# Two-block transformer kernel on one core: order of emission in the gated delta net's pair loop

## Chip, cores and metric

One core of a Trainium2 chip runs the whole program; times are device microseconds of that core. TensorE (PE in the profile) multiplies, VectorE (DVE) and ScalarE (ACT) work on tiles, GpSimd (POOL) does small side work, SyncE (SP) issues most transfers.

## What is computed

Two transformer blocks one after the other on x of 512 tokens by 1024 features. The first has dilated attention and retention, cross attention and a gated MLP. The second takes h = modulated norm of x, and hc the same of 256 context tokens, and runs a gated delta net (GDN) and latent attention (MLA) side by side, merges them and adds an MLP. The change is in the GDN: 8 heads of 128, in both directions, over chunks (of 128 tokens in the kernel, 6 of them: 2 of context, 4 of x). The core of the reference:

```python
qkv = jax.nn.silu(_centred_conv(qkv, conv_w))          # 5 taps
q, k = _l2norm(q), _l2norm(k)
...
diff = gc[..., :, None] - gc[..., None, :]
decay = jnp.where(tri, jnp.exp(jnp.where(tri, diff, 0.0)), 0.0)
a_mat = jnp.where(strict, jnp.einsum('bhnid,bhnjd->bhnij', kb, k) * decay, 0.0)
t_mat = lax.linalg.triangular_solve(eye + a_mat, jnp.broadcast_to(eye, a_mat.shape), ...)
u = jnp.einsum('bhnij,bhnjd->bhnid', t_mat, vb)
w = jnp.einsum('bhnij,bhnjd->bhnid', t_mat, kb * jnp.exp(gc)[..., None])
qk = jnp.where(tri, jnp.einsum('bhnid,bhnjd->bhnij', q, k) * decay, 0.0)
...
def step(s, inp):
    v_new = u_i - jnp.einsum('bhcd,bhde->bhce', w_i, s)
    o_i = einsum(qd_i, s) + einsum(qk_i, v_new)
    s = s * gl_i[..., None, None] + einsum(kd_i, v_new)
...
y = _rms(o, w_norm) * jax.nn.silu(z)
```

## The kernel before

Products of weights are made in three parts (`mm3s`): each operand is a high and a low half, and a product of one 128-feature tile with the 512 tokens of x is 24 instructions of 512 columns on lines 234, 235 and 237 (8 blocks of 128 rows, three parts each); with the 256 context tokens 24 of 256 columns. Weight halves come in two ways. Keys, queries and values have theirs laid ready in memory ("parts") and only load them (`whi<-parts`). Those of z and of all that follows load raw (`wraw`); ACT makes whi (L178), DVE wlo (L179). Both ways have two buffers of each name. The 512-column results go to two banks `pg`, others to four banks `sc` and two `pt`.

`gdn` goes over four pairs of heads, numbered 0 to 3. A pair's work, by the names used below:

- keys, queries (512 columns only) and values: two feature tiles each. A tile's product is evacuated twice by ACT (L1247, L1248), DVE adds the four other taps of the conv (`conv`, L1254, 510/511 or 254/255 columns), ACT applies silu (L1256). Keys and values are turned (L1284; evacuated on L1286, L1289), keys and queries get their norms (L1309, L1322, L1325). `betas` takes the logarithm of the key norms (L1341).
- the within-chunk part, first half of `states`: products of keys with keys and queries (L1364, L1366), a decay mask per direction from two small products (L1373, L1374) through an exponential on ACT (L1376), products with it on DVE (L1378 to L1380), and the diagonal 32x32 blocks of all into X (L1384, L1386).
- the inversion, on DVE alone: a transpose of X (L1390), 31 steps of small multiplications and subtractions (L1398, L1401, some 124 instructions), two transposes back (L1403, L1404).
- TT: small products on PE that put the inverse of the blocks together (L1418 to L1456); then the recurrence of six steps (L1475 to L1527), in which PE, DVE and ACT wait for each other at each step. L1502 is the last product of a step.
- `output`: z's two products, their silu (L1535), the norm of O (L1542 to L1547), O turned on PE (L1550) and multiplied with z (L1552).

SP runs in program order. On the other engines a list scheduler sets the order: it takes the instructions by a planner's costs, and among those that are ready what was emitted first goes first. So the order in which the code emits a pair's parts decides what fills PE while DVE inverts. Before, the loop emits: TT, recurrence and all before it of pair p (`states`), then keys, queries and values of pair p + 1 (`inputs`), `betas`, then z and the output of pair p. In the last pass `tail()` stands in place of the next inputs: it holds the latent projections of MLA (256-column weight pieces, loaded raw; results evacuated on L980) and gates. The list of the calls:

```python
*inp, n2 = inputs(0)
g = next(gg)
...
for pair in range(4):
    O = states(pair, *inp, *bt)
    ...
    output(pair, O, sq_)
```

`gg` is a generator of the decay gates (`gdn_gates`, L1150 on), of which `inputs(0)` takes the first stage between its query norms and the turn of its values.

Of the kernel before, what the change touches and what calls it, by code (L numbers as in the profile page):

```python
# [75 lines left out]
class Kernel:  # L76
# [1155 lines left out]
    def gdn(self, H, HC, w, tail):  # L1232
# [8 lines left out]
        def conv(ps, tile):  # L1241

            raw, acc = (self.page([sum(p.shape[1] for p in ps)]) for _ in range(2))
            o = 0
            for p in reversed(ps):
                n = p.shape[1]
                act(raw[:, o:o + n], p, AF.Copy)  # L1247
                act(acc[:, o:o + n], p, AF.Copy, scale=cw[:, 48 + tile:49 + tile])  # L1248
                for i in (0, 1, 3, 4):
                    wi = cw[:, 24 * i + tile:24 * i + tile + 1]  # L1250
                    a, b = max(0, 2 - i), min(n, n + 2 - i)
                    y = acc[:, o + a:o + b]
                    v = raw[:, o + a + i - 2:o + b + i - 2]
                    dve.scalar_tensor_tensor(y, v, wi, y, op0=OP.mult, op1=OP.add)  # L1254
                o += n
            act(acc, acc, AF.Silu)  # L1256
            return acc, raw
# [11 lines left out]
        def feat(f0, both, first=None):  # L1269

            W, pc = first or (None, None)
            W = W or self.weights(w, 0, 8, f0, 256)
            for f in range(2):
                r = [product(W, H, f, 512, "pg")]
                if both:
                    r.append(pc[f] if pc else product(W, HC, f, 256, "pg"))
                yield r
# [15 lines left out]
        def inputs(pair):  # L1293


            h0 = 2 * pair
            qT, sq_, kT, ktok, vtok = ([] for _ in range(5))
            fk = fv = None
            if pair == 0:
                fv = None, ahead(2048)[1]  # L1300
                fk = ahead(1024)
            kc = [conv(ps, 8 + h0 + f) for f, ps in enumerate(feat(1024 + pair * 256, True, fk))]
            n2, root = [], []
            for f, (c, raw) in enumerate(kc):
                kt = self.page([6, 128])
                turn(c, kt)
                ss = self.tmp.tile([128, 6], F32, name="kss")
                for t in range(6):
                    act(raw[:, t * 128:t * 128 + 128], kt[:, t], AF.Square, accum_out=ss[:, t:t + 1])  # L1309
                n2.append(self.hb.tile([128, 6], F32, name=f"kn2{f}", bufs=2))  # L1310
                root.append(self.hb.tile([128, 6], F32, name=f"krt{f}", bufs=2))
                nc.gpsimd.tensor_scalar(n2[f], ss, 1e-6, None, op0=OP.add)
                r = self.hb.tile([128, 6], F32, name="krs", bufs=2)
                nc.gpsimd.tensor_tensor(r, n2[f], self.mhalf[:, :6], op=OP.pow)
                nc.gpsimd.tensor_tensor(root[f], r, n2[f], op=OP.mult)
                kT.append(c.rearrange("p (a b) -> p a b", a=6))
                ktok.append(kt)
            qc = [conv(ps, h0 + f) for f, ps in enumerate(feat(pair * 256, False))]
            vc = [conv(ps, 16 + h0 + f) for f, ps in enumerate(feat(2048 + pair * 256, True, fv))]
            for q, sq in qc:  # L1320
                qT.append(q)
                act(sq, q, AF.Square)  # L1322
                pq = self.bank([128, 4], "pt")
                for t in range(4):
                    mm(pq[:, t:t + 1], sq[:, t * 128:t * 128 + 128], ones, start=True, stop=True)  # L1325
                s1 = self.tmp.tile([128, 4], F32, name="qss")
                dve.tensor_copy(s1, pq)
                sq_.append(self.rstd(s1, 1.0 / 128, 128e-6, "qrs"))
            if pair == 0:
                next(gg)  # L1330
            for f, (c, _) in enumerate(vc):
                vt = self.page([6, 128])
                turn(c, vt, root[f])
                vtok.append(vt)
            return qT, sq_, kT, ktok, vtok, n2

        def betas(pair, n2):
            h0, nb, bd = 2 * pair, [], []
            for f in range(2):
                ln = self.hb.tile([128, 6], F32, name="kln", bufs=2)  # L1340
                act(ln, n2[f], AF.Ln)  # L1341
                inv = self.hb.tile([128, 6], F32, name="kin", bufs=2)
                dve.reciprocal(inv, n2[f])
                for out, nm, v, op in ((nb, "nb", ln, OP.subtract), (bd, "bd", inv, OP.mult)):
                    out.append(self.hb.tile([128, 6, 2], F32, name=f"k{nm}{f}", bufs=2))
                    dve.tensor_tensor(out[f], g[nm][:, :, h0 + f::8], v[:, :, None].to_broadcast([128, 6, 2]), op=op)
            return nb, bd

        def states(pair, qT, sq_, kT, ktok, vtok, nb, bd):
            h0 = 2 * pair  # L1350
            D2 = range(2)
            lane = {(h, d): slice(12 * h + 6 * d, 12 * h + 6 * d + 6) for h in D2 for d in D2}

            def blk(b):
                return slice(32 * b, 32 * b + 32)


            E, M = {}, {}
            for h in range(2):
                pg = [self.bank([128, n, 128], "sc") for n in (2, 4)]  # L1360
                pk = self.bank([128, 4, 128], "sc")
                for c in range(6):
                    k = kT[h][:, c]
                    mm(pg[c >= 2][:, c - 2 * (c >= 2)], k, k, start=True, stop=True)  # L1364
                    if c >= 2:
                        mm(pk[:, c - 2], k, qT[h][:, (c - 2) * 128:(c - 1) * 128], start=True, stop=True)  # L1366
                for d in range(2):
                    i = d * 8 + h0 + h
                    ec, e = self.page([2, 128], s="w"), self.page([4, 128], s="w")
                    for a, n in ((0, 2), (2, 4)):  # L1370
                        pe = self.bank([128, n, 128], "sc" if a else "pt")
                        pf = pe.rearrange("p a b -> p (a b)")
                        mm(pf, sel[:, i:i + 1].to_broadcast([64, 128]), g["rows"][:, a * 128:(a + n) * 128], start=True, stop=False)  # L1373
                        mm(pe, idb, msk[:, d, None, :].to_broadcast([128, n, 128]), start=False, stop=True)  # L1374
                        for c in range(n):
                            act((e if a else ec)[:, c], pe[:, c], AF.Exp, bias=nb[h][:, a + c, d:d + 1])  # L1376
                    m = self.page([6, 128], s="w")
                    dve.tensor_tensor(m[:, :2], ec, pg[0], op=OP.mult)  # L1378
                    dve.tensor_tensor(m[:, 2:], e, pg[1], op=OP.mult)
                    dve.tensor_tensor(e, e, pk, op=OP.mult)  # L1380
                    for b in range(4):
                        xb, mb = X[blk(b), lane[h, d]], m[blk(b), :, blk(b)]
                        if d == 0:
                            act(xb, mb, AF.Copy)  # L1384
                        else:
                            dve.transpose(xb, mb)  # L1386
                    E[h, d], M[h, d] = e, m


            dve.transpose(L, X.rearrange("p n i -> p i n"))  # L1390
# [15 lines left out]

            pairs = [[(2 * p + d, 2 * p + 1 - d) for p in D2] for d in D2]
            h1 = [slice(64 * d, 64 * d + 64) for d in D2]
            h2 = h1[::-1]
            V, TT, pa, P, pb = ([None, None] for _ in range(5))  # L1410
            for h in D2:
                V[h] = [[R[:, lane[h, d]] for R in ((R1, R2), (R2, R1))[d]] for d in D2]
                pa[h] = self.bank([128, 6, 32], "sc")
                for c in range(6):
                    for p in D2:
                        for d in D2:
# [46 lines left out]
            O = [self.page([4, 128], s="w") for h in range(2)]  # L1463
            for s in range(6):
# [22 lines left out]
                for h in range(2):  # L1487
                    if s < 5:
                        vd[h] = self.hb.tile([128, 2, 128], F32, name="gvd", bufs=2)
                        f = bd[h].rearrange("p c d -> p (c d)")[:, lo:hi + 1:hi - lo]  # L1490
# [63 lines left out]
                self.dbg(f"d_o{h0 + h}", f)  # L1554

        gg = self.gdn_gates(H, HC, w)
        *inp, n2 = inputs(0)
        g = next(gg)
        g = next(gg)
        bt = betas(0, n2)  # L1560
        for pair in range(4):
            O = states(pair, *inp, *bt)
            sq_ = inp[1]
            if pair < 3:
                *inp, n2 = inputs(pair + 1)
                bt = betas(pair + 1, n2)
            else:
                tail()
            output(pair, O, sq_)
# [54 lines left out]
```

## Time and profile before

| | us |
|---|---|
| median of three runs (2303.47 to 2306.6) | 2304.15 |
| the profiled execution | 2301.69 |
| its span, first to last instruction | 2299.6 |
| PE busy in the span | 2180.8 (95%) |
| DVE busy | 1193.7 (52%) |
| ACT busy | 990.1 (43%) |
| POOL busy | 255.3 (11%) |

The mean granted TensorE clock over the span is 0.984 of full speed. The page's slices show PE at nine tenths or more nearly everywhere; the GDN stands from about 940 to 1480 us. Busy shares over the whole span hide which engine ends a wait, so the rows further down are of that stretch.

### The profile page before, as it was taken

What the parts mean: (1) busy time and instruction counts of PE and PEld (TensorE: products, weight loads), DVE (VectorE), ACT (ScalarE), POOL (GpSimd) and SP (SyncE); (2) the same over time, 40 slices, a digit from 0 to 9 for tenths busy, and PEclk for the clock granted to TensorE, in tenths of its full rate; (3) what the DMA queues carried; (4) which work ended last, traced back from release to release, by engine and by line L of the source; (5) the groups of instructions that cost most, each with busy time, mean ns of one, the idle gap of its engine ahead of it and who ended that gap; (6) DMA issues with size and microseconds to landing.
All of it is one profiled execution on the core that took longest, in us unless ns stands there. A gap on an engine that the chain in (4) does not pass through costs nothing.

```text
span 2299.6 us, 38173 instructions
## 1 busy us (share of the span) xinstructions
PE 2180.8 (95%) x15367; PEld 1941.2 (84%) x15367; DVE 1193.7 (52%) x2628; ACT 990.1 (43%) x2054; POOL 255.3 (11%) x419
## 2 busy tenths in 40 slices
PE   8999999998899999888989897999999998999999
PEld 8889978888779889767878786888988898898988
DVE  4554444555443233559696867336775454434343
ACT  4443234545333233565555654445555324313231
POOL 0221100001000001201111110211210001010112
PEclk9999999999999999999999998999999998999999
DMA  5233485455663322422121310230112442323232
GB/s 173 80 128 130 159 290 194 158 183 183 216 231 104 101 92 97 152 80 93 47 92 47 98 47 15 90 120 28 30 51 92 165 147 74 101 83 101 93 100 92
DMA packets 195816, 262.05 MB, mean 114 GB/s; under 512 B 12343, under 2 KB 157495, under 8 KB 195639
## 3 DMA queue, kind: packets, MB, share of 16 engines
q1 hardware_dynamic: 188864, 244.61, 33.0%
q10 hardware_dynamic: 6775, 15.00, 1.8%
q8 instruction: 120, 1.97, 0.3%
q14 instruction: 57, 0.47, 0.1%
HBM read 223.39 MB, written 36.18 MB: 113 GB/s over the span
## 4 chain that ended last, share of the span: by engine, by line
PE 74%; issue 9%; DMA 5%; DVE 5%; ACT 4%; POOL 2%; ACTq 0%; SPq 0%; POOLq 0%; DVEq 0%
PE pg L234 15%; PE pg L235 15%; PE pg L237 15%; PE sc L234 4%; PE sc L237 4%; PE sc L235 4%; DMA whi<-parts 2%; DMA parts<-fraw 1%; PE pg L223 1%; PE pg L224 1%; PE pg L225 1%; PE pa L1148 1%; PE sc L465 1%; DMA wraw<-in_w_kv_mem 1%; PE sc L1486 1%
## 5 line engine op out<-in xcount | busy, mean ns | idle before, releaser
L179 DVE TENSOR_TENSOR wlo<-wraw,whi 128x1024 fp32r<-128x1024 f32 (+2 forms) x267 | 325.7, 1222 | 415.2 <-ACT whi L178 411.3
L234 PE MATMUL pg<-xhi,whi 128*128 128x512 f32 (+1 forms) x1104 | 426.9, 390 | 32.5 <-DMA whi<-parts 13.4
L178 ACT ACTIVATE whi<-wraw 128x1024 fp32r<-128x1024 f32 (+2 forms) x267 | 275.5, 1034 | 417.7 <-PE pg L235 352.2
L235 PE MATMUL pg<-xlo,whi 128*128 128x512 f32 (+1 forms) x1104 | 424.9, 388 | 0.0
L237 PE MATMUL pg<-xhi,wlo 128*128 128x512 f32 (+1 forms) x1104 | 291.2, 384 | 0.9 <-DMA wlo<-parts 0.9
L234 PEld LDWEIGHTS pg<-xhi,whi 128*128 128x128 f32 x1104 | 210.5, 191 | 79.6 <-ACT whi L178 14.4
L235 PEld LDWEIGHTS pg<-xlo,whi 128*128 128x128 f32 x1104 | 210.7, 191 | 37.0
L237 PEld LDWEIGHTS pg<-xhi,wlo 128*128 128x128 f32 x1104 | 202.7, 190 | 41.2 <-DMA wlo<-parts 3.1
L234 PE MATMUL pg<-whi,xhi 128*128 128x256 f32 (+1 forms) x608 | 158.8, 291 | 0.3 <-ACT a L980 0.3
L235 PE MATMUL pg<-whi,xlo 128*128 128x256 f32 (+1 forms) x608 | 157.0, 289 | 0.0
L234 PE MATMUL sc<-whi,a 128*128 128x256 f32 x560 | 141.7, 285 | 1.6 <-ACT whi L178 1.6
L235 PE MATMUL sc<-whi,a 128*128 128x256 f32 x560 | 141.2, 284 | 0.0
L234 PE MATMUL pg<-whi,a 128*128 128x256 f32 x560 | 140.9, 283 | 0.0
L235 PE MATMUL pg<-whi,a 128*128 128x256 f32 x560 | 140.8, 283 | 0.0
L234 PEld LDWEIGHTS pg<-whi,xhi 128*128 128x128 f32 x608 | 118.4, 195 | 4.5 <-ACT whi L178 2.5
L235 PEld LDWEIGHTS pg<-whi,xlo 128*128 128x128 f32 x608 | 118.2, 194 | 1.1 <-issue 0.8
L237 PE MATMUL pg<-wlo,xhi 128*128 128x256 f32 (+1 forms) x608 | 103.2, 289 | 14.4 <-DVE wlo L179 14.4
L234 PEld LDWEIGHTS sc<-whi,a 128*128 128x128 f32 x560 | 107.7, 192 | 2.0 <-ACT whi L178 1.8
L235 PEld LDWEIGHTS sc<-whi,a 128*128 128x128 f32 x560 | 107.7, 192 | 0.2
L234 PEld LDWEIGHTS pg<-whi,a 128*128 128x128 f32 x560 | 107.5, 192 | 0.2
L235 PEld LDWEIGHTS pg<-whi,a 128*128 128x128 f32 x560 | 107.5, 192 | 0.0
L1254 DVE SCALAR_TENSOR_TENSOR a<-a,convw,a 128x510 f32<-128x510 f32 (+3 forms) x160 | 98.5, 640 | 15.1 <-ACT a L1248 14.1
(475 smaller groups left out, 4496.5 us busy)
## 6 DMA issues: line engine op xcount, KB each, us to landing
wraw<-in_w_in SPq DMA_DIRECT2D x56, 512.0 KB, 5.7
fraw<-in_w_mod SPq DMA_DIRECT2D x48, 512.0 KB, 5.9
parts<-fraw SPq DMA_DIRECT2D x48, 512.0 KB, 3.9
wraw<-in_w_gate_up SPq DMA_DIRECT2D x44, 512.0 KB, 4.3
wraw<-in_w_mlp_in SPq DMA_DIRECT2D x32, 512.0 KB, 4.4
wraw<-in_w_mlp_out SPq DMA_DIRECT2D x32, 512.0 KB, 3.3
whi<-parts SPq DMA_DIRECT2D x26, 512.0 KB, 3.9
wlo<-parts SPq DMA_DIRECT2D x26, 512.0 KB
```

The lines of the kernel that those rows point to most:

```text
L178: nc.scalar.activation(hi, raw, AF.Copy)
L179: self.wlo_eng.tensor_tensor(lo, raw, hi.bitcast(F32), op=OP.subtract)
L223: mm(out, a[0], b[0], start=start, stop=False)
L224: mm(out, a[0], b[1], start=False, stop=False)
L225: mm(out, a[1], b[0], start=False, stop=stop)
L234: mm(out, A[k][0], B[k][0], start=start and k == 0, stop=False)
L235: mm(out, A[k][late], B[k][1 - late], start=False, stop=False)
L237: mm(out, A[k][1 - late], B[k][late], start=False, stop=stop and k == n - 1)
L465: nc.tensor.matmul(po[h][:, i], pT[:, j], v[:, j, h * 64:h * 64 + 64], start=j == 0, stop=j == i)
L1148: nc.tensor.transpose(pt[:, s, i * 128:i * 128 + 128], p2[i][:, (2 * s2 + s) * 128:(2 * s2 + s) * 128 + 128], self.ident)
L1254: dve.scalar_tensor_tensor(y, v, wi, y, op0=OP.mult, op1=OP.add)
L1486: mm(kv[h][:, at[d], 0], M[h, d][:, c], r[h, d], start=True, stop=True)
```

## The change

`inputs` ends with the queries; the values get a function of their own (`values`), and the first half of `states` becomes `within`. The loop calls them in the order keys and queries, `betas`, `within`, `values` of the next pair, then `output` of the pair at hand. Ahead of the loop, the gates are made in one go behind `inputs(0)`, then `betas(0)`, `within(0)` and `values(0)`. No instruction's work changes. Lines of `within` and TT lie 4 to 8 further down in the new file (L1368 for L1364, L1380 for L1376, L1398 for L1390, L1426 for L1418), of `output` 8 (L1558 for L1550).

```diff
@@ inputs
-            vc = [conv(ps, 16 + h0 + f) for f, ps in enumerate(feat(2048 + pair * 256, True, fv))]
...
-            if pair == 0:
-                next(gg)
-            for f, (c, _) in enumerate(vc):
+            return (qT, kT, ktok), (root, sq_), n2, fv
+
+        def values(pair, root, fv):
+
+            vtok = []
+            for f, ps in enumerate(feat(2048 + pair * 256, True, fv)):
+                c, _ = conv(ps, 16 + 2 * pair + f)
                 vt = self.page([6, 128])
                 turn(c, vt, root[f])
                 vtok.append(vt)
-            return qT, sq_, kT, ktok, vtok, n2
+            return vtok
@@ states
-        def states(pair, qT, sq_, kT, ktok, vtok, nb, bd):
+        def within(pair, qT, kT, nb):
...
                     E[h, d], M[h, d] = e, m
+            return E, M
+
+        def states(pair, qT, kT, ktok, vtok, bd, E, M):
+            h0 = 2 * pair
@@ the loop
-        *inp, n2 = inputs(0)
-        g = next(gg)
-        g = next(gg)
-        bt = betas(0, n2)
+        keys, rest, n2, fv = inputs(0)
+        for g in gg:
+            pass
+        nb, bd = betas(0, n2)
+        EM = within(0, *keys[:2], nb)
+        vtok = values(0, rest[0], fv)
         for pair in range(4):
-            O = states(pair, *inp, *bt)
-            sq_ = inp[1]
+            O = states(pair, *keys, vtok, bd, *EM)
+            sq_ = rest[1]
             if pair < 3:
-                *inp, n2 = inputs(pair + 1)
-                bt = betas(pair + 1, n2)
+                keys, rest, n2, fv = inputs(pair + 1)
+                nb, bd = betas(pair + 1, n2)
+                EM = within(pair + 1, *keys[:2], nb)
+                vtok = values(pair + 1, rest[0], fv)
```

**PE, where O of pair 1 is turned.** Before, the within-chunk products of pair 2 follow it (L1366 key by query, L1364 key by key, then mask products):

```order
L237 MATMUL pg<-xhi,wlo 128x512 x4
L1550 MATMUL pt<-ident,w_11911 128x128 x4
L1550 MATMUL pt<-ident,w_11912 128x128 x4
L1366 MATMUL sc<-a_12399,a_12238 128x128
L1364 MATMUL sc<-a_12238 128x128
L1366 MATMUL sc<-a_12399,a_12238 128x128
L1364 MATMUL sc<-a_12238 128x128
```

In the new order the same turn (L1558 now) is followed by a weight product of 512 columns, of the keys of pair 3:

```order
L237 MATMUL pg<-xhi,wlo 128x512 x4
L1558 MATMUL pt<-ident,w_11911 128x128 x4
L1558 MATMUL pt<-ident,w_11912 128x128 x4
L234 MATMUL pg<-xhi,whi 128x512
L235 MATMUL pg<-xlo,whi 128x512
L234 MATMUL pg<-xhi,whi 128x512
```

The within-chunk products of pair 2 have moved ahead of z and of the values of their own pair.

**ACT, at the exponentials of pair 2** (`w<-sc` and `w<-pt` are the masks). Before, the silus of z (L1535), the stores of the output (L1553) and one table load stand ahead of them:

```order
L1256 ACTIVATE a_12565<-a_12565 128x768
L1535 ACTIVATE a_12686<-pg 128x512
L1289 ACTIVATE a_12618<-pt,krt_12360 128x128 x6
L1535 ACTIVATE a_12713<-pg 128x512
L1553 DMA od<-a_12686 128x512
L1553 DMA od<-a_12713 128x512
L1376 ACT_TABLE_LOAD
L1376 ACTIVATE w_12780<-pt,knb_12637 128x128 x2
L1376 ACTIVATE w_12781<-sc,knb_12637 128x128 x4
```

In the new order (L1380 is the exponential, L1344 the logarithm of the key norms, L1256 a silu behind a conv, L1321 the square of a query):

```order
L1344 ACT_TABLE_LOAD
L1344 ACTIVATE kln<-kn_12359 128x6
L1256 ACT_TABLE_LOAD
L1256 ACTIVATE a_12399<-a_12399 128x512
L1247 ACTIVATE a_12432<-pg 128x512
L1248 ACTIVATE a_12433<-pg,convw 128x512
L1321 ACTIVATE a_12398<-a_12399 128x512
L1550 ACTIVATE junk,on_12855<-w_11912 128x128
L1380 ACT_TABLE_LOAD
L1380 ACTIVATE w_12495<-sc,knb_12469 128x128 x4
L1256 ACT_TABLE_LOAD
L1256 ACTIVATE a_12433<-a_12433 128x512
```

The queries' evacuation and silu now stand among the logarithms and exponentials, with a table load at each change of function.

**DVE, at the end of the inversion of pair 3** (L179 is the low half of the tail's first weights). Before:

```order
L1398 TENSOR_TENSOR invt_9503<-inv 128x45
L1398 TENSOR_TENSOR invt_9504<-inv 128x30
L179 TENSOR_TENSOR wlo<-wraw,whi 128x1024
L1401 TENSOR_TENSOR inv<-inv,invt_9503 128x3x15
L1401 TENSOR_TENSOR inv<-inv,invt_9504 128x2x15
L179 TENSOR_TENSOR wlo<-wraw,whi 128x1024
```

In the new order (the inversion's steps are L1406 and L1409):

```order
L1406 TENSOR_TENSOR invt_9503<-inv 128x30
L179 TENSOR_TENSOR wlo<-wraw,whi 128x1024
L1406 TENSOR_TENSOR invt_9504<-inv 128x30
L1409 TENSOR_TENSOR inv<-inv,invt_9503 128x2x15
L179 TENSOR_TENSOR wlo<-wraw,whi 128x1024
L1409 TENSOR_TENSOR inv<-inv,invt_9504 128x2x15
```

Both low halves stand at the same place of the inversion, within its last steps.

## Rows read from the trace of the kernel before

**Rows 1.** Busy time by window: us, then each engine's busy time, clock, DMA share, GB/s.

```profile
core 0: us, PE busy (x) PEld busy (x) DVE busy (x) ACT busy (x) POOL busy (x), PEclk, DMA share, GB/s
940.00:1480.00 540.00, 485.31 (x4218) 418.15 (x4218) 370.54 (x1116) 309.40 (x871) 85.46 (x153) 0.97 0.24 73
1219.65:1289.46 69.81, 64.98 (x345) 53.06 (x344) 52.85 (x182) 33.65 (x93) 9.06 (x16) 0.98 0.38 116
...
1380.00:1400.00 20.00, 4.66 (x27) 4.18 (x26) 19.93 (x88) 1.21 (x4) 1.01 (x3) 0.66 0.14 40
```

**Rows 2.** PE's waits, 940 to 1480 us: total, times, longest.

```profile
PE pg L237 <- DVE wlo L179: 14.4, 1, 14.4
PE pg L234 <- DMA whi<-parts: 13.4, 12, 2.2
PE pg L234 <- ACT a L1248: 5.3, 6, 1.3
```

**Rows 3.** PE's timeline at pairs 0, 2, 3: start, length, instruction, idle before.

```profile
1017.44 0.82 PE L1224 MATMUL pt<-ident,a 128*64 128x128 f32 x6 [1.16 <-DVE g_nb L1212]
...
1219.65 0.71 PE L1502 MATMUL sc<-gvn,w 128*128 128x128 f32 x4
...
1251.99 0.39 PE L1374 MATMUL sc<-gmask,idb 128*128 128x512 bf16 x1
...
1289.46 0.31 PE L1418 MATMUL sc<-inv,w 32*32 32x32 f32 x4
...
1332.73 0.71 PE L1502 MATMUL sc<-gvn,w 128*128 128x128 f32 x4
...
1394.57 1.22 PE L237 MATMUL pg<-wlo,xhi 128*128 128x256 f32 x4 [14.39 <-DVE wlo L179]
...
1398.87 0.28 PE L1418 MATMUL sc<-inv,w 32*32 32x32 f32 x4 [0.95 <-DVE inv L1403]
```

**Rows 4.** The chain that ended last, 1228 to 1240 us.

```profile
1229.36 0.23 PE pg L234
```

**Rows 5.** DVE's timeline at the inversions of pairs 2 and 3.

```profile
1257.17 2.07 DVE L1390 STREAM_TRANSPOSE inv<-inv 128x1024 f32<-128x1024 f32 x1
...
1288.64 1.17 DVE L1254 SCALAR_TENSOR_TENSOR a<-a,convw,a 128x255 f32<-128x255 f32 x2
...
1371.90 2.08 DVE L1390 STREAM_TRANSPOSE inv<-inv 128x1024 f32<-128x1024 f32 x1
...
1393.29 1.22 DVE L179 TENSOR_TENSOR wlo<-wraw,whi 128x1024 fp32r<-128x1024 f32 x1
...
1398.63 1.96 DVE L1404 STREAM_TRANSPOSE inv<-inv 128x1024 f32<-128x1024 f32 x1
```

**Rows 6.** Line L1374, last mask products: lengths, first and last start.

```profile
L1374 PE MATMUL sc<-gmask,idb x16: 389/390/390, 1020.8 to 1365.9; 128*128 128x512 bf16 x16
```

**Rows 7.** ACT's groups by shape, 940 to 1440 us: busy, mean ns, idle before.

```profile
L1309 ACT ACTIVATE a<-a 128x128 f32<-128x128 f32 x48 | 14.2, 303 | 0.1
...
L1256 ACT ACT_TABLE_LOAD x9 | 11.5, 1283 | 11.5 <-DVE a L1254 11.5
...
L1341 ACT ACT_TABLE_LOAD x5 | 6.4, 1283 | 0.1
...
L1376 ACT ACT_TABLE_LOAD x3 | 3.8, 1283 | 5.9 <-DVE a L1552 5.9
```

**Rows 8.** ACT's timeline at a table load and at exponentials.

```profile
1200.26 1.28 ACT L1341 ACT_TABLE_LOAD   x1
1201.56 0.21 ACT L1341 ACTIVATE kln<-kn 128x6 f32<-128x6 f32 x1
...
1251.67 2.17 ACT L1376 ACTIVATE w<-sc,knb 128x128 f32<-128x128 f32 x8 [3.35 <-PE sc L1374]
```

**Rows 9.** DVE's groups by shape, 1035 to 1400 us.

```profile
L1254 DVE SCALAR_TENSOR_TENSOR a<-a,convw,a 128x511 f32<-128x511 f32 x36 | 27.0, 753 | 0.0
...
L179 DVE TENSOR_TENSOR wlo<-wraw,whi 128x1024 fp32r<-128x1024 f32 x10 | 12.2, 1224 | 3.6 <-ACT whi L178 3.5
L1254 DVE SCALAR_TENSOR_TENSOR a<-a,convw,a 128x254 f32<-128x254 f32 x24 | 11.4, 476 | 0.4 <-ACT a L1248 0.4
```

More of the change, by code (lines that the diff above doesn't have):

```diff
@@ L1296, in inputs @@
             h0 = 2 * pair
-            qT, sq_, kT, ktok, vtok = ([] for _ in range(5))
+            qT, sq_, kT, ktok = ([] for _ in range(4))
             fk = fv = None
@@ L1347, in betas, with blk @@
             return nb, bd
-        def states(pair, qT, sq_, kT, ktok, vtok, nb, bd):
+        D2 = range(2)
+        lane = {(h, d): slice(12 * h + 6 * d, 12 * h + 6 * d + 6) for h in D2 for d in D2}
+        def blk(b):
+            return slice(32 * b, 32 * b + 32)
+        def within(pair, qT, kT, nb):
             h0 = 2 * pair
[L1351 to L1355, printed above, removed]
             E, M = {}, {}
```

## Prediction

> **What bounds the kernel now.** I read the busy time by window first. From 940 to 1480 us, the stretch that the change rewrites, TensorE (PE) is busy 485.3 of 540 us, VectorE (DVE) 370.5 and ScalarE (ACT) 309.4 [rows 1]. So PE bounds it, 54.7 us of it lie idle, and a new order can win no more than these, plus what the half clock behind a wait costs. The table of waits says where they lie: 14.4 us in one wait for a low weight half from DVE, 13.4 us in 12 waits for parted weights, 5.3 us in 6 waits for ACT's evacuations, and many of 1 to 3 us [rows 2].
>
> The timeline puts the large one in pair 3. The four products on wlo start at 1394.57, after PE stood still for 14.39 us [rows 3]; their 1.22 us are 0.30 each for half-width products, whose full rate is about 0.115 (half of a 512-wide one's 0.23) [rows 3, 4], and the granted clock of 1380 to 1400 is 0.66 [rows 1]. The wlo comes from DVE at 1393.29, at the tail of the inversion, which began with L1390 at 1371.90 and ends with L1404 at 1398.63 plus 2 [rows 5]. In the other pairs PE arrives just as DVE ends: in pair 2 L1390 starts at 1257.17, the conv behind L1404 at 1288.64 [rows 5], and the first TT product (L1418) at 1289.46 with no wait shown [rows 3].
>
> Three dates of each pair matter below: the end E of the recurrence before it, T0 (the last mask product, L1374), and the first L1418. Pair 2 has E at 1219.65 + 0.71 = 1220.4, T0 at 1251.99 and L1418 at 1289.46: E to T0 31.6, E to L1418 69.1 us. Pair 3 has 1333.4, 1365.9 and 1398.87: 32.5 and 65.4 us [rows 3, 6].
>
> **What the change moves.** It adds and removes no product, conv or weight load. Each pair's within part is emitted ahead of its values, and the values ahead of the z of the pair before. What must lie beside the 31 us inversion is no longer keys, queries and half the values of the next pair, but the second value tile, z and the first keys. I counted PE's instructions between E and L1418 in both orders, at 0.23 us for a 512-wide product, 0.115 for a half-wide one, 0.11 for a 128-wide one and 0.2 to 0.4 for selections and masks: 57.7 before and 61.6 after in pair 2; 43.8 and 54.3 in pair 3. So before, 69.1 - 57.7 = 11.4 us are lost between E and L1418 in pair 2 and 21.6 in pair 3. The question is whether L1418 comes later by more than 3.9 and 10.5 us.
>
> *Within part, on ACT.* Before, the within part came after z: its exponentials stood together behind one table load (L1376 has 3 loads in three pairs, the silus of L1256 9, the logarithms of L1341 5 [rows 7]). In the new order the remaining logarithms, silus of keys and queries and the exponentials alternate just there: the two queries' squares and silus stand between exponentials, with 8 loads from E to the first value's silu. The whole program has 40 loads for 31. One is 1.28 us, and the next activation starts 1.30 us after it (1200.26, 1201.56) [rows 8]; nine are 11.7 us. ACT's row in pair 2, from E to the second query's evacuation: some 40 instructions whose lengths add up to 21 us, 18 with their overlaps (12 key squares of 0.30 with a read-out each [rows 7] are the largest part, four loads the next). From that evacuation to the last exponential: 1.3 evacuation, 3 loads 3.8, 24 exponentials at 0.27 (2.17 for 8 [rows 8]) 6.5, copies into the inversion's input 2.9, silu, squares and the first value tile's evacuation 4.5, together 19. So the last exponential ends near E + 37, T0 lies near E + 36 and L1390 near E + 41.5; before it started at 1257.17, E + 36.8 [rows 5]. That is 4.7 later.
>
> The Trainium skill (ScalarE: Activation LUTs, What ACT_TABLE_LOAD costs) gives 1283 ns for a load, which the trace agrees with, and 1380 ns of drain on top, which no gap here shows; the page's 2.66 us would make nine of them about 24 us, and by Table sets: the hidden batching unit of the same page one batches activations by set, which this order does less than the one before. I go by the 1.30.
>
> *Inversion, on DVE.* From L1390 to the conv behind L1404 it takes 31.5 in pair 2 with 11 convs of 0.4 to 0.7 between [rows 5, 9] and 28.7 in pair 3 with two wlo of 1.22. Afterwards pairs 1 and 2 have fewer convs there (the values' eight instead), but two wlo of z (2.4), two norm products L1555 (0.7 each) and two L1560: 31 to 33. L1418 of pair 2 is due at E + 73 to 75, against 69.1 with 3.9 more work: 0 to 2 lost, I take **+1.0**. Pair 1 has the same chain, with six convs between the last X transposes and the inversion: six at 0.39 to 0.66 are 3.3 us later, with cover for about 2: **+1.4**, between 0 and 3.
>
> *Pair 0.* Beside the gates' chain (three table loads and DVE) stood products of the first values: 13 of them between L1205 and the first mask product at 0.23, 3.0 us, around a wait of 1.16 [rows 3]. These products move behind the within part, and 20 key and query products of 0.11 come in their place. Bounds 0 and 4; I take **+2**, since the chain is ACT's and DVE's and nothing makes it shorter.
>
> *Pair 3 and the 14.4 us.* One expects the change to fill them: z, its wlo and the second value tile now lie beside that inversion, 22.1 us of PE work from T0 to the first need of the tail's wlo, where there were 14.5 (1365.9 to 1380.2). But the tail's two wlo keep their place, behind all but the last steps of the inversion, and the inversion itself gets longer: eight convs 4.2, two wlo 2.4, two L1555 and two L1560 2.6 [rows 9], about 9 us. Before, the wlo was there 28.7 after T0; now it is at about 37.6, and PE waits 10 to 15 again (part of it as earlier waits in PE's row, for the evacuations behind ACT's whi and loads). L1418 comes at T0 + 42 for 33.0, T0 at E + 36 for 32.5: 12.5 later with 10.5 more work done: **+2**, between -3 and +4.
>
> *Waits exchanged.* The DMA waits of 13.4 us [rows 2] belong to weights that follow each other on one pair of buffers; the loads are the same and in the same order, so they move. Behind each new stall PE starts again at the lower level, as in 1380 to 1400, where the granted clock is 0.66 [rows 1]: per restart 1 to 1.5 us, against 1 to 1.7 behind the short DMA waits of before. For three pairs I take **+1**.
>
> Sum: 2 + 1.4 + 1.0 + 2 + 1 = **+7.4 us**. The profiled execution takes 2301.69 us, 2.09 over its span; 2309.1 after the change. The median of the runs, 2304.15, is 2.5 above the profiled one, so I predict **2311 us**. No-change means within 0.2%, 4.6 us, of 2304.15; about that is what a measurement of this kernel can tell.
>
> **Rivals.**
> *The hole closes.* If the tail's wlo comes to DVE before the inversion is deep in it (its whi is ready early, and DVE's row might only look as it does), or if ACT is not late, pair 3 loses 14.4 less, plus 2 of half clock: 2304 - 16 = 2288. The row of DVE speaks against it: wlo stands near the inversion's end in both orders. A half of it (L1390 not later than before, stall 5 or less) gives 2296. It decides when the wlo is ready less than 24 us after T0.
> *Everything is hidden.* PE waits at the end of the inversion in any case, so work moved ahead of it is only waiting moved; later inversion and longer cover cancel: 2304, within 4.6. For it speaks that before, the four pairs too lose 10 us each, whatever lies there.
> *ACT becomes the bound.* With in-order engines each exponential that is late holds its bank, the mask product for that bank holds the value products behind it on PE, and these hold the evacuations. If half of the 8 loads in each of three pairs delays PE by 1 us, 12 us come on top: 2323. For it: ACT is busy 33.6 of 69.8 us in pair 2 [rows 1] and the loads come in the 37 us where it is nearly full. Against it: 36 us of every 69.8 ACT is idle, and the values' products need it only for their evacuation.
>
> By the price of a switch on the page named above this rival would be the case; the two rows 1.30 us apart speak against that price.
>
> **How the numbers follow.** Chances: my sum 0.38, ACT bound 0.17, hidden 0.22, hole closed wholly or by half 0.23. Of the sum's own range (2306 to 2316) little lies within 4.6 of before; so slower 0.54, same 0.23, faster 0.23. Its own range is 2306 to 2316. The terms' bounds add up to about -3 and +14 (2301 to 2318); towards the rivals I leave out the best of the hole's cases and the worst of ACT's: 2294 to 2324.
>
> **What would show it.** Right: the first waits of PE for a wlo of L179 stand at 8 to 15 us behind pair 3's inversion, whose L1398 (L1390 before) to L1412 takes 36 to 38 us; E to L1398 about 41 us in pairs 2 and 3; 9 more loads in ACT's rows; 54.7 idle us grown by 5 to 10. Wrong: no PE wait over 5 us in 1300 to 1480, or E to L1398 at 37 or less, or an inversion in pair 3 no longer than 31 us: then the hole's filling has worked and the time is below 2300.

## The result and the profile after

The changed kernel is slower, by 1.0 to 1.1%. Three executions took 2323.12, 2329.68 and 2332.48 us, against a median of 2303.81 before; ratio 1.0103, 95% interval 1.0082 to 1.0125. Another four had a median of 2329.99 (2326.11 to 2331.84), ratio 1.0115 (1.0087 to 1.0144). That is +24 and +26 us, where I had forecast +7. A fourth execution of the first set, of 4246.88 us (with it the median is 2331.08), and one of e14 below, of 4098.12, are left out of all that follows: in the first, the 512-wide products took 679 ns on the mean for 394, throughout the program. The trace read here is of an execution of 2326.11 us, span 2324.3, mean clock 0.976 (before 0.984).

Busy time of the changed kernel by window (columns as in [rows 1]). The first line is the whole stretch; the other five run from 940 to the first L1426 of each pair, and on to 1480:

```profile
940.00:1480.00 540.00, 476.34 (x4067) 408.05 (x4066) 360.48 (x1086) 305.02 (x830) 73.70 (x132) 0.94 0.22 67
940.00:1062.50 122.50, 104.13 (x542) 82.29 (x540) 79.99 (x246) 65.00 (x162) 14.78 (x29) 0.92 0.31 99
1062.50:1165.96 103.46, 90.86 (x846) 77.22 (x845) 81.09 (x255) 64.43 (x191) 17.66 (x32) 0.95 0.18 57
1165.96:1288.97 123.01, 110.42 (x926) 92.62 (x926) 84.83 (x263) 72.21 (x198) 16.92 (x30) 0.93 0.21 65
1288.97:1406.96 117.99, 100.21 (x893) 86.12 (x894) 87.58 (x263) 72.58 (x197) 18.70 (x33) 0.93 0.22 68
1406.96:1480.00 73.04, 70.72 (x864) 69.80 (x865) 26.98 (x63) 30.81 (x86) 5.64 (x12) 0.95 0.10 31
```

What TensorE lost here is not only what it idled. Idle time rose from 54.7 us [rows 1] to 63.7, by 9.0; the granted clock fell from 0.97 to 0.94, and 0.03 of 540 us are 16 more. The two make up the 25 us between the spans.

For a single stage I count as lost what PE idled, and half of the time in which it was busy while the granted clock was 0.50. The mean clock of a stage does not do for this, since it also counts time in which PE idled at the lower clock: in 1380 to 1400 before [rows 1], 15.3 us idle and 0.34 x 20 would be 22 us out of 20. In the first stage of the changed kernel the clock is 0.50 in three spans:

```profile
940.00:941.53 1.53, 1.53 (x10) 1.53 (x9) 0.13 (x1) 1.50 (x7) 1.10 (x4) 0.50 0.71 281
996.14:1006.38 10.24, 7.49 (x27) 5.93 (x28) 3.44 (x21) 4.47 (x10) 0.69 (x2) 0.50 0.08 31
1040.52:1047.34 6.82, 5.55 (x13) 4.41 (x14) 6.82 (x36) 2.28 (x7) 0.00 (x0) 0.50 0.00 0
```

So 18.4 idle and half of 14.6, 25.7, are lost there. Before, the same stage has 14.0 idle and 0.7 us of work at the lower clock, 14.4:

```profile
940.00:1065.29 125.29, 111.27 (x613) 88.96 (x612) 83.98 (x256) 69.14 (x168) 12.64 (x25) 1.00 0.41 129
```

| lost on TensorE up to L1418/L1426 of | before | after | difference | of it by the clock | forecast |
|---|---|---|---|---|---|
| pair 0 | 14.4 | 25.7 | +11.3 | +6.9 | +2 |
| pair 1 | 11.9 | 16.6 | +4.7 | +0.8 | +1.4 |
| pair 2 | 10.1 | 20.1 | +9.9 | +5.8 | +1.0 |
| pair 3 | 22.0 | 23.4 | +1.3 | +2.2 | +2 |
| on to 1480 | 6.6 | 5.3 | -1.3 | +1.2 | 0 |

(The forecast had a further +1 for waits exchanged in the pairs 1 to 3.) PE's waits of the changed kernel, 940 to 1480, in total, times, longest:

```profile
PE pg L234 <- ACT a L1248: 14.2, 9, 2.3
PE pt L1284 <- ACT a L1256: 12.8, 5, 4.0
PE pg L237 <- DVE wlo L179: 9.0, 1, 9.0
PE pg L234 <- DMA whi<-parts: 7.3, 5, 2.3
```

Against [rows 2] the second row is new: the turn of a value tile waits for its silu. The first grew from 5.3, and the wait for the tail's low half shrank from 14.4 to 9.0. What happens in pair 2 is seen on three engines. PE:

```profile
1250.22 0.64 PE L237 MATMUL pg<-hc,wlo 128*128 128x256 f32 x4
1254.85 0.91 PE L1284 MATMUL pt<-ident,a 128*128 128x128 f32 x6 [3.99 <-ACT a L1256]
1257.90 0.79 PE L234 MATMUL pg<-xhi,whi 128*128 128x512 f32 x1 [2.14 <-ACT a L1248]
1258.49 0.63 PE L235 MATMUL pg<-xlo,whi 128*128 128x512 f32 x1
1258.91 0.63 PE L234 MATMUL pg<-xhi,whi 128*128 128x512 f32 x1
...
1262.82 0.39 PE L234 MATMUL pg<-xhi,whi 128*128 128x512 f32 x1
1263.05 0.39 PE L235 MATMUL pg<-xlo,whi 128*128 128x512 f32 x1
```

DVE at the same place:

```profile
1249.30 0.75 DVE L1254 SCALAR_TENSOR_TENSOR a<-a,convw,a 128x511 f32<-128x511 f32 x1
1249.97 1.98 DVE L1398 STREAM_TRANSPOSE inv<-inv 128x1024 f32<-128x1024 f32 x1
1251.88 0.70 DVE L1254 SCALAR_TENSOR_TENSOR a<-a,convw,a 128x510 f32<-128x510 f32 x1
```

and ACT:

```profile
1252.66 1.28 ACT L1256 ACT_TABLE_LOAD   x1 [1.18 <-DVE a L1254]
1253.95 0.84 ACT L1256 ACTIVATE a<-a 128x768 f32<-128x768 f32 x1
1255.54 1.66 ACT L1289 ACTIVATE a<-pt,krt 128x128 f32<-128x128 f32 x6 [0.75 <-PE pt L1284]
1257.06 0.42 ACT L1247 ACTIVATE a<-pg 128x256 f32<-128x256 f32 x1
```

Read it from DVE on. The last tap of the first value tile's conv runs at 1251.88, behind mask products, the transposes into X and the first transpose of the inversion. Only then does ACT load a table for its silu. The turn starts at 1254.85; it stands right behind the second value tile's product in PE's row, so that PE had nothing else to do for 3.99 us. The second tile's evacuation stands behind the turn's in ACT's row, so its bank stays taken and z's product waits 2.14 us more. From there a 512-wide product starts every 0.43 us, half rate, until 1262.82, where it is every 0.23 again: 12 products take 4.9 us for 2.7, so 2.2 are lost. One such stall costs 8.3 us. Pairs 0, 1 and 3 have the same one with waits of 3.1 + 2.2, 2.6 + 2.3 and 2.8 + 2.2 us, and in all four the granted clock is 0.50 for 6.8 us.

The inversion lasts longer too: from the start of L1398 to the end of L1412 it takes 32.8, 36.1, 40.7 and 38.4 us in pairs 0 to 3; before it took 31.7, 31.7, 31.6 and 28.7. DVE's groups inside that of pair 2 (1249.97 to 1290.7), and one row of its timeline:

```profile
L1409 DVE TENSOR_TENSOR inv<-inv,invt 128x110 f32<-128x110 f32 (+35 forms) x61 | 12.6, 248 | 0.0
L1406 DVE TENSOR_TENSOR invt<-inv 128x110 f32<-128x110 f32 (+35 forms) x61 | 12.6, 245 | 0.0
L1254 DVE SCALAR_TENSOR_TENSOR a<-a,convw,a 128x511 f32<-128x511 f32 (+3 forms) x12 | 6.8, 597 | 4.0 <-ACT a L1248 3.9
L179 DVE TENSOR_TENSOR wlo<-wraw,whi 128x1024 fp32r<-128x1024 f32 x2 | 2.4, 1214 | 0.0
L1560 DVE SCALAR_TENSOR_TENSOR a<-pt,onw,a 128x512 f32<-128x512 f32 x2 | 1.4, 748 | 1.7 <-PE pt L1558 1.7
...
1286.23 0.48 DVE L1254 SCALAR_TENSOR_TENSOR a<-a,convw,a 128x254 f32<-128x254 f32 x1 [3.94 <-ACT a L1248]
```

The steps cost what they did, and there are 12 conv instructions, as before. New are two low halves of z (2.4), two products of the output (1.4) and 5.6 us in which DVE stands still among the steps: 1.7 until O is turned, and 3.9 at 1286.23 before a conv of the next keys, until ACT has evacuated their product. That product comes late in PE's row, behind the stall above and a wait of 2.01 us for weights at 1277.95; how much of the 3.9 is due to which is not shown. In pairs 1 and 3 DVE stands still for 1.1 and 0.8 us only.

### The profile page after: what moved, and what is told of

It reads as the page before. It is cut to its first block, busy times and chain, and to the rows that moved or that the text cites. A ratio compares the mean times of both kernels' runs of the same rounds, so it can differ in the third digit from the quotient of the medians.

```text
span 4245.1 us, 38196 instructions
## 1 busy us (share of the span) xinstructions
PE 4197.0 (99%) x15367; PEld 3424.7 (81%) x15367; DVE 1204.0 (28%) x2628; ACT 1021.9 (24%) x2063; POOL 259.8 (6%) x419
## 4 chain that ended last, share of the span: by engine, by line
PE 98%; ACT 1%; DVE 1%; DMA 0%; issue 0%; ACTq 0%; POOLq 0%; POOL 0%; DVEq 0%
PE pg L234 20%; PE pg L235 20%; PE pg L237 20%; PE sc L234 5%; PE sc L235 5%; PE sc L237 5%; PE pg L223 2%; PE pg L224 2%; PE pg L225 2%; PE fl L753 1%; PE sc L1494 1%; PE pa L1148 1%; PE sc L1483 1%; PE sc L1507 1%; PE sc L465 1%; PE sc L1510 1%
## 5 line engine op out<-in xcount | busy, mean ns | idle before, releaser
L234 PE MATMUL pg<-xhi,whi 128*128 128x512 f32 (+1 forms) x1104 | 727.9, 662 | 11.3 <-ACT a L1248 11.3
L235 PE MATMUL pg<-xlo,whi 128*128 128x512 f32 (+1 forms) x1104 | 726.6, 660 | 0.0
L179 DVE TENSOR_TENSOR wlo<-wraw,whi 128x1024 fp32r<-128x1024 f32 (+2 forms) x267 | 319.5, 1197 | 1154.9 <-ACT whi L178 710.0
L237 PE MATMUL pg<-xhi,wlo 128*128 128x512 f32 (+1 forms) x1104 | 557.1, 657 | 0.0
L178 ACT ACTIVATE whi<-wraw 128x1024 fp32r<-128x1024 f32 (+2 forms) x267 | 276.5, 1036 | 1157.7 <-PE pg L235 1059.2
L234 PEld LDWEIGHTS pg<-xhi,whi 128*128 128x128 f32 x1104 | 333.6, 303 | 175.6 <-issue 142.3
L235 PEld LDWEIGHTS pg<-xlo,whi 128*128 128x128 f32 x1104 | 333.8, 303 | 155.7 <-issue 141.6
L234 PE MATMUL sc<-whi,a 128*128 128x256 f32 x560 | 240.8, 439 | 1.6 <-ACT whi L178 1.6
L234 PE MATMUL pg<-whi,a 128*128 128x256 f32 x560 | 240.9, 441 | 0.0
L235 PE MATMUL pg<-whi,a 128*128 128x256 f32 x560 | 240.7, 440 | 0.0
L235 PE MATMUL sc<-whi,a 128*128 128x256 f32 x560 | 240.6, 439 | 0.0
L235 PEld LDWEIGHTS pg<-whi,a 128*128 128x128 f32 x560 | 197.3, 352 | 0.0
L234 PEld LDWEIGHTS pg<-whi,a 128*128 128x128 f32 x560 | 197.0, 352 | 0.2 <-ACT whi L178 0.2
L234 PEld LDWEIGHTS sc<-whi,a 128*128 128x128 f32 x560 | 194.6, 347 | 2.8 <-ACT whi L178 2.5
L235 PEld LDWEIGHTS sc<-whi,a 128*128 128x128 f32 x560 | 195.3, 349 | 1.0 <-issue 0.8
L237 PEld LDWEIGHTS pg<-wlo,xhi 128*128 128x128 f32 x608 | 161.0, 348 | 8.0 <-DVE wlo L179 7.2
```

What stands on the lines that cost most here:

```text
L178: nc.scalar.activation(hi, raw, AF.Copy)
L179: self.wlo_eng.tensor_tensor(lo, raw, hi.bitcast(F32), op=OP.subtract)
L234: mm(out, A[k][0], B[k][0], start=start and k == 0, stop=False)
L235: mm(out, A[k][late], B[k][1 - late], start=False, stop=False)
L237: mm(out, A[k][1 - late], B[k][late], start=False, stop=stop and k == n - 1)
```

## Experiments

The theories that the expectations name: A, the prediction's, ACT's row delays the inversion; B, restarts at half clock are the loss; C, pair 0 is. Theory D came from the first trace: the stall of the value turn shown above. Ratios are to the kernel before, run in between on the same chip. K, Q and V are keys, queries and values; the diffs show the emission in outline. E is the end of the recurrence.

**The changed kernel again.** 

> The changed kernel again, for its trace. Its runs were 2323 to 2332 us. Theory A (ACT's row: logarithms, silus and exponentials alternate and the inversion starts late) expects recurrence end to L1398 at 41 us or more in pairs 2 and 3. Theory B (restarts: more short PE waits, each with products at half clock behind it) expects a granted clock of 0.94 or less in 1000 to 1480, and at least 8 us lost by slow products. Theory C (pair 0: the gates' chain has no value products beside it) expects L1426 of pair 0 at least 6 us later than L1418 before.

1.0115 (1.0087 to 1.0144). B's signs are there: clock 0.94, and 17 us more by slow products. So are A's: L1398 of pairs 2 and 3 stands 47.0 and 41.9 us behind E. C's is not: L1426 of pair 0 stands at 1062.5, where L1418 stood at 1065.3, though with much less work done.

**The three moves apart.** The change does three things: the within part goes ahead of z, the values go behind the within part, and pair 0 is emitted in the new order. Three kernels with pair 0 as before:

```diff
 e1:  K, Q, V; betas
+     within(p + 1)
      output(p)
-     within(p + 1)
 e2:  K, Q; betas; within(p + 1); V; output(p)      (loop as in the change)
 e3:  K, Q; betas; output(p); within(p + 1); V
```

> Pair 0 as before; in the loop keys, queries and values stand as before, only the within part moves ahead of z. 48 table loads, 31 before. Theory A expects the worst time of all, 2335 or more, since the loads grow by 17. Theory B expects 2310 to 2330. Theory C expects 2304, as pair 0 is untouched.

> Pair 0's emission as before, the loop as in the change. 41 table loads. Theories A and B expect most of the loss to stay, 2320 to 2330; Theory C expects the time of before, 2304 to 2310.

> Pair 0 as before; in the loop keys and queries, then z and the output of the pair at hand, then the within part, then the values: only the values move behind the within part. 34 table loads. Theory A expects 2304 to 2308, since the exponentials stand together again. Theory B expects 2310 or more if the values' products come with as many waits. Theory C expects 2304.

| | values ahead of within | values behind within |
|---|---|---|
| z ahead of within | before: 1 | e3: 1.0101 (1.0073 to 1.0129) |
| within ahead of z | e1: 0.9956 (0.9939 to 0.9973) | e2: 1.0045 (1.0025 to 1.0066) |

(In e3 the values stand behind z as well.) In microseconds: the within part ahead of z wins 10 with the values ahead and 13 with them behind; the values behind the within part cost 23 and 20. The change's pair 0 adds the rest, from 1.0045 to 1.0115, 16 us. So theory A falls, that the loads in ACT's row are the loss: e1 has the most table loads (48) and is the fastest kernel of all, 2292.23 us, faster than both. No turn waits for a silu in its trace, and the tail's low half is waited for 2.4 us:

```profile
PE pg L234 <- DMA whi<-parts: 10.4, 8, 2.3
PE sc L1457 <- issue: 6.1, 3, 2.5
PE pg L234 <- ACT whi L178: 4.9, 1, 4.9
PE pg L234 <- ACT a L1248: 4.2, 4, 1.3
...
PE pg L237 <- DVE wlo L179: 2.4, 2, 1.3
```

In e2 the values cost their 20 us in another way than in the change. No turn waits for its silu there, but PE waits 15.2 us for evacuations (L1248). In ACT's row the evacuation of a value tile stands behind the exponentials (L1390 there), and these wait for the mask products on PE; in pair 3, ACT and then PE:

```profile
1350.09 2.18 ACT L1390 ACTIVATE w<-sc,knb 128x128 f32<-128x128 f32 x8 [2.81 <-PE sc L1388]
1352.11 1.48 ACT L1398 ACTIVATE inv<-w 32x192 f32<-32x192 f32 x4
1353.61 0.38 ACT L1247 ACTIVATE a<-pg 128x256 f32<-128x256 f32 x1
...
1354.53 0.79 PE L234 MATMUL pg<-xhi,whi 128*128 128x512 f32 x1 [3.61 <-ACT a L1248]
```

**Pair 0 alone**, the loop as before:

```diff
-        keys, rest, n2, vtok = inputs(0)          (values inside)
+        keys, rest, n2, fv = inputs(0); gates; betas(0)
+        EM = within(0, ...); vtok = values(0, ...)
```

> The change at pair 0 alone (gates in one go, then the within part, then the values); the loop as before. From the lost time of TensorE up to the first L1426 (28.2 us after, 14.0 before) Theory D expects 2304 + 14, so 2313 to 2322. The prediction's term for pair 0 was 2 us: 2304 to 2308.

1.0041 (1.0026 to 1.0056): +9.4 us. Up to L1436 (L1426 of the change, here at 1063.29) its trace has 17.0 us idle and 15.3 us of work at the lower clock, so 24.6 lost for 25.7 in the change and 14.4 before.

**What is late in the stall.** Before, both value convs and the query norms stood between a value tile's conv and its turn; in `values` each turn follows its own conv at once. Three edits of the changed kernel: the turns of the loop's values behind the output; the value convs without their side taps (DVE); the values' silu as a copy (ACT). The last two leave work out, so they compute something else.

```diff
 e4:             vc = values(pair + 1, ...)
                 output(pair, O, sq_)
+                vtok = turned(vc, rest[0])
 e5:  -          for i in (0, 1, 3, 4):            e6:  -  act(acc, acc, AF.Silu)
      +          for i in ():                           +  act(acc, acc, AF.Copy)
```

> As the change, but in the loop the turns of the value tiles are emitted behind the output of the pair at hand, not behind each value conv. Theory D (in the changed kernel TensorE meets the first value tile's turn right behind the second's product; its silu is late, the second tile's evacuation then stands behind the turn's, z's product waits for the bank, and all restarts at half clock) expects these waits of 2.6 to 4.0 and 2.2 us to be gone from pairs 1 to 3 and the time at 2305 to 2315. Theory A (the inversion is late and longer; these waits only take its place) expects 2325 to 2332.

> As the change, but the values' conv leaves out its four side taps, so VectorE has 8 instructions less per value tile. Theory D with VectorE as what is late expects the waits of the turn at 1.5 us or less in each pair and the time at 2300 to 2312. With ScalarE's table load as what is late: waits of 2 to 4 us stay, time above 2320.

> As the change, but the values' silu is a copy, so that no table load stands between the exponentials and the turn. Theory D with VectorE as what is late expects each turn's wait shorter by the load's 1.3 us only, time 2315 to 2326; with ScalarE as what is late: waits gone, 2300 to 2312.

e4 1.0042 (1.0032 to 1.0053), e5 0.9997 (0.9983 to 1.0011), e6 1.0057 (1.0038 to 1.0077): 17, 27 and 13 us better than the change. (e4 has both turns of pair 0 behind both convs as well.) The times fall in the ranges of theory D with DVE as what is late, e6 at the edge of its range. e5 has no wait of a turn for its silu left; its first waits are

```profile
PE pg L234 <- ACT a L1248: 7.6, 5, 1.8
PE pg L234 <- DMA whi<-parts: 6.2, 7, 2.2
PE pg L237 <- DVE wlo L179: 5.4, 1, 5.4
```

and its inversions are back at 28.9 to 32.3 us. But e5 also takes 64 instructions off DVE, so not all of its 27 us need be the stall's. And e6, with ACT alone relieved, wins half as much: the waits of turns fell from 12.8 to 5.4 us, more than the 1.3 of a load each, so the silu and its load are a part of the chain. e6 has 40 loads like the change; those that went from L1256 came back ahead of z's silu (L1543).

**Do the repairs add up?** e9: pair 0 as before and the late turns. e13: late turns in pair 0 alone.

```diff
 e9:  start of the kernel before; loop of e4
 e13: -  for f, ps in ...: c = conv(...); turn(c, ...)
      +  both convs of pair 0, then both turns
```

> The change with both repairs: pair 0 emitted as before, and in the loop the turns of the values behind the output. Theory D, whose two parts are pair 0 (about 14 us) and the turns (about 17), expects them to add up: 2296 to 2304. If they share a cause (a late pair 0 makes the rest late), the time stays at 2306 to 2314.

> The changed kernel, in which only pair 0's values are turned behind both value convs; the loop as in the change. If the 17 us that the late turns won came from the loop: 2326 or more. If from pair 0 (the wait of 3.1 and 2.2 us there): 2312 to 2318. If from both, half and half: 2318 to 2325.

They don't. e13 1.0095 (1.0074 to 1.0117): of e4's 17 us about 5 are pair 0's, by ratios whose intervals overlap. e9 1.0088 (1.0071 to 1.0105), worse than e2 with its turns in place. A reason why it wins nothing is in e2's trace: with pair 0 as before the scheduler had put the loop's turns elsewhere, none waits for its silu, and 15.2 us of waits for L1248 stand in their place (e9: 15.6). The late turns had nothing to take away. Why e9 is 10 us worse than e2 I can't say.

**The wait for the tail's low half.** e8: the kernel before, with only pair 3's within part ahead of z.

```diff
+            if pair == 2: EM = within(3, ...)
             output(pair, O, sq_)
```

> The kernel before, with the within part of pair 3 alone ahead of z of pair 2. If the gain of the kernel with all within parts first (about 10 us) came from pair 3, where z now lies beside the inversion and the 14.4 us wait is gone, this one gains as much: 2288 to 2297. If it came from pairs 1 and 2 (inversions that start earlier): 2300 to 2305.

0.9984 (0.9971 to 0.9997), 4 us of e1's 10, between the two forecasts: the wait of 14.4 fell to 3.3 in two, and a wait of 4.6 for a whi of L178 took part of the place. Then five kernels that make some low halves on GpSimd:

```diff
 e10, e11, e12 (change, before, e1), in the tail:
+            self.wlo_eng = nc.gpsimd if f0 == 0 else nc.vector
 e14 (before):    ... if f0 == 256 ...
 e15 (change):    the same for z's weights
```

> The changed kernel, with the two low halves of the tail's first weights made on GpSimd, so that they don't stand in VectorE's row behind the inversion of pair 3. The wait of 9.0 us there should be gone. If that wait and its restart are lost time of TensorE: 2330 less 9 to 13, so 2317 to 2321. If the inversion's end holds TensorE in any case: 2327 or more.

> The same edit on the kernel before, where the wait is 14.4 us. If it is lost time: 2302 less 14 to 18, so 2284 to 2289. If the inversion's end holds TensorE in any case: 2298 or more.

> The same edit on the kernel with all within parts first and the values ahead of them, whose waits for this low half are 2.4 us together: 2288 to 2292, and the least time of all if the gains add up.

> The kernel before, with the low halves of the tail's second weights (those that the 14.4 us wait is for, as the run with the first ones on GpSimd showed) made on GpSimd. If the wait is lost time: 2302 less 12 to 18, so 2284 to 2290. If the inversion's end holds TensorE in any case: 2298 or more.

> The changed kernel, with the low halves of z's weights made on GpSimd, 2.4 us less on VectorE at the start of the inversions of pairs 1 to 3. If VectorE's row there is what makes the loop late, 2318 to 2326; if not, 2328 or more.

e10 1.0083 (1.0061 to 1.0105): 7 us of the 9.0, with intervals that overlap. e11 0.9989 (0.9977 to 1.0002): the edit missed its aim, since the wait of the kernel before is for the second weights, and stayed at 12.0. e12 0.9973 (0.9960 to 0.9986), 2297.35 us, above its forecast and no better than e1. e14 took the right ones: 0.9980 (0.9961 to 0.9998), 4.6 us of 14.4. In its PE row the wait is gone, and another stands 20 us further on:

```profile
1379.09 0.74 PE L237 MATMUL pg<-wlo,xhi 128*128 128x256 f32 x4 [0.88 <-POOL wlo L179]
1381.42 0.74 PE L237 MATMUL pg<-wlo,xhi 128*128 128x256 f32 x4 [0.63 <-POOL wlo L179]
1400.52 0.39 PE L1419 MATMUL sc<-inv,w 32*32 32x32 f32 x4 [6.22 <-DVE inv L1404]
```

The inversion's end had stood behind the low half. (That inversion is 2.0 us longer than before, by GpSimd's work beside it, as the last section shows; so some of the 6.22 is the edit's own.) e15 1.0104 (1.0068 to 1.0140): nothing won. But DVE was not relieved by it: beside GpSimd's low halves in pair 1, two pairs of its steps, 0.33 us a pair elsewhere, took 2.46 and 2.50. So e15 leaves it open whether z's low halves in DVE's row make the loop late.

## Why the prediction was wrong

The direction was right, in part by luck, and what bounds the kernel was right; the time lies above the range. The move that I had priced as a cost, the within part ahead of z, wins 10 to 13 us. The loss comes from the values behind it (20 to 23) and from pair 0 (9 to 16), for whose chains I had no term of this size.

*Pair 0.* "Bounds 0 and 4; I take +2" is the first step that failed: its edit alone costs 9.4 us (6 to 13), and 11.3 by lost time in the change. I had costed the gates' chain and nothing behind it. Of the 11.3, 6.9 are clock and 4.4 idle. The clock had fallen at 996.14, among small products behind a wait of 1.05 us, and stayed at 0.50 to 1006.38, through the gates' wait of 2.60 us at 1000.25 (L1202; before, the chain's wait was 1.16, at L1224 [rows 3]). Then comes the value turn's 3.06 and 2.23, again with half rate; late turns there won about 5 us (e13). The values lay beside the gates before, and their conv beside nothing urgent; now it stands among the inversion's first steps, and ACT waits 5.35 us for it at 1037.79.

*Within part, on ACT.* The inversion does start later (E + 47.0 and 41.9 in pairs 2 and 3 for 41.5), but a late start alone need not cost: e5 has E + 47.7 and 46.7 and takes the time of before, and e1 has E + 41.0 and 40.2, more loads, and wins. My reading that 11.4 us are lost there in pair 2 was too high as well: [rows 1] has PE busy 65.0 of the 69.8 us. The difference of work that I went by does not hang on it.

*Inversion, on DVE.* "31 to 33" was 36.1 and 40.7 in pairs 1 and 2. It does not follow from my own items either: those that I added in pair 3 (eight convs 4.2, two low halves 2.4, L1555 and L1560 2.6) make 35.5 on an inversion without other work, 28.7 - 2.4. In pair 2 the waits in DVE's row come on top, 5.6 us, which I had left out. Its first L1426 stands at E + 86.0, where I had it due at E + 73 to 75.

*Waits exchanged, +1.* This term was mis-sized about as much as pair 0's: outside pair 0 the clock took 10 us more. I held that new restarts cost what the old ones did. But of the old waits, those of 0.96 and 1.16 us were followed by products at full rate, and of the three of 2.1 to 2.2 for weights two by 3.4 us at the lower clock. The new pairs of waits, 2.6 to 4.0 and 2.1 to 2.3 us with a turn between, were each followed by 4.5 to 5.6 us of products at half rate. Nor does a restart always follow a wait: the clock had fallen ahead of the wait of 2.60.

*Pair 3.* Right in kind: the tail's low half kept its place at the inversion's end, and PE waited 9.0 us for it, 10 to 15 forecast; the inversion took 38.4, 36 to 38 forecast; the stage lost 1.3 more, 2 forecast. That the wait is mostly waiting moved (e14: 4.6 of 14.4) speaks for the rival "everything is hidden" as far as this wait goes; the rival "the hole closes" priced it at 16.

*The rival "ACT becomes the bound"* gave 2323, near the time but for another reason. Its chain, evacuations held behind other work on ACT and products behind them, is what the traces show. But the loads do not start it: in the changed kernel the value conv on DVE does, as far as e5 and e6 tell, and in e2 the exponentials behind their mask products do.

## What to carry to other kernels

When work is moved beside a long serial stretch of one engine, ask not only whether there is enough of it, but what each piece waits for. z's products need their weight halves beforehand and nothing in between. A value tile goes from TensorE through an evacuation, a conv on the very VectorE that inverts, and a silu before TensorE can turn it; with the turn right behind, TensorE waits for the whole chain, and late turns alone brought 17 us back. An order that is changed in one go is better taken apart: here its three moves were worth -10 to -13, +20 to +23 and +9 to +16 us, and the first alone is a faster kernel. And a stall is to be priced with the slow products behind it, by the rows behind waits of its own length.

## What I had not expected of the hardware

GpSimd and VectorE hold each other up. A low half of 128x1024 took GpSimd 2.39 us in e11, and a VectorE instruction on 128x4, 0.16 us elsewhere, took 2.35 beside it:

```profile
1350.23 2.39 POOL L179 TENSOR_TENSOR wlo<-wraw,whi 128x1024 fp32r<-128x1024 f32 x1
1350.29 2.35 DVE L1544 TENSOR_TENSOR on<-qrs 128x4 f32<-128x4 f32 x1 [0.82 <-POOL qrs L246]
```

In e14 two low halves took GpSimd 2.4 us each, and two pairs of the inversion's steps beside them took 2.6 us each, where the pairs around them take 0.4:

```profile
1376.61 4.75 POOL L179 TENSOR_TENSOR wlo<-wraw,whi 128x1024 fp32r<-128x1024 f32 x2 [29.04 <-ACT whi L178]
1376.26 0.37 DVE L1399 TENSOR_TENSOR invt<-inv 128x78 f32<-128x78 f32 x2
1376.56 2.58 DVE L1402 TENSOR_TENSOR inv<-inv,invt 128x78 f32<-128x78 f32 x2
1379.05 2.60 DVE L1399 TENSOR_TENSOR invt<-inv 128x100 f32<-128x100 f32 x2
1381.57 0.42 DVE L1402 TENSOR_TENSOR inv<-inv,invt 128x100 f32<-128x100 f32 x2
```

So the inversion of pair 3, rid of two low halves of 1.22 us, took 30.7 us instead of 28.7, 4.4 more than its own work. It goes the other way too: in e10 the first of two low halves took 5.34 us while VectorE's steps ran at their usual length, the second 2.44.

The Trainium skill (SBUF — State Buffer, Terms) has the two engines share a pair of ports, which one holds for a whole instruction while the other waits. The traces agree: what was taken off VectorE came back as its waiting.
